# A decoder layer on one core: memory between attention and mixer laid out anew, the mixer's first weights split beside the last projection tiles, the down projection's maxima queued behind other reads

## Chip, cores and metric

One core of one Trainium2 chip. The metric is the device time in microseconds of one execution. Its engines are TensorE (PE, with its weight loads as PEld), VectorE (DVE), ScalarE (ACT), GpSimd (POOL) and SyncE (SP); DMA transfers are issued here from SP's and ACT's queues. Each engine takes its instructions in the order in which they were laid down when the program was built.

## The reference

One layer on x (2048 tokens, 1024 wide), all float32: a token mixer of four head groups (RWKV-7, mLSTM, sliding-window attention, forgetting attention), whose outputs are concatenated and projected, and then a gated MLP. The change lies between the last attention and the end of the MLP:

```python
y = jnp.concatenate([y_a, y_b, y_c, y_d], axis=-1).astype(dt)
x = x + _rmsnorm(y @ w_out[l], norm_mix_post[l]).astype(dt)
h = _rmsnorm(x, norm_ffn_pre[l]).astype(dt)
gate, up = jnp.split(h @ ffn_w_up[l], 2, axis=-1)
gate = _causal_dwconv(gate, ffn_conv_w[l], ffn_conv_b[l])
f = jax.nn.gelu(gate, approximate=True) * up
x = x + _rmsnorm(f @ ffn_w_down[l], norm_ffn_post[l]).astype(dt)
```

w_out is 1024 x 1024, ffn_w_up 1024 x 5632, ffn_w_down 2816 x 1024, the convolution has width 3.

## The kernel before

Every float32 operand of a large product is split into two float16 parts (a leading part and a residual, scaled by a power of two taken from its largest magnitude), and a product is three products of parts. The largest magnitude of a weight block needs a maximum along the rows (VectorE) and one over the partitions (GpSimd, partition_all_reduce).

**Attention (fox).** 16 items (head, token chunk of 512) in sequence. An item has a front (products of queries and keys, row maxima fmx on VectorE) and a back (products again, exponentials on ACT, residuals fhl on VectorE or GpSimd, products with the values). The front of an item is interleaved with the back of the one before it. Chunk c needs c+1 key blocks (ka and kb), loaded from ACT's queue into a ring of buffers, whose number is the first argument of fox_pools: 8 in the second half. The last four items are those of chunk 3.

**Output projection.** o_tiles(c) does the four tiles of 128 tokens of chunk c: o_front loads y, takes its maximum, splits it and transposes it by DMA (yt); o_back makes 96 products with Wo, normalises, adds x, normalises again and transposes the result into U2[c], the float16 parts of the mixer's input (V0 to V3 in the trace). Tiles of chunks 0 and 1 run beside attention; the last four tiles need the last four items.

**Mixer.** The up projection uses a two by two scheme with seven products of blocks instead of eight: combine(p) builds the sums and differences of the blocks of U2 of two chunks, split into float16 parts, T0 for p = 0 and T1 for p = 1. A unit of it (eight in each) is 4 sums on GpSimd, 4 subtractions and a residual on VectorE and a cast on ACT. For each of the 22 weight blocks j, up_weights(j) loads 1 MB (raw), takes its maximum, and makes four sums on GpSimd (S); up_split makes the float16 parts Wup (two buffers, w_n). ffn_up(p, j) is a pass: 84 products of 512 columns into three banks (psa, psb, psc, each double), evictions on ACT and VectorE (line 1656), convolution, GELU, the product F on GpSimd, and a write to DRAM (fD). The order of the passes is (0,0), (0,1), (1,0), (1,1), then (0,j), (1,j) for j = 2 to 21. up_weights also loads the block j of the down projection's weights (rd) and takes its maximum mD (line 1620).

**Down projection.** It reloads weights (wdr) and F (fr), splits both and makes 2112 products; the scale of all weights comes from the 22 maxima mD.

**Order and memory.** The planner of the tile framework orders each engine's instructions greedily in a simulated timeline: an instruction goes as soon as its inputs and its memory are free, earlier program text first. issue_after(mark) keeps instructions of the same engine behind the instruction mark. Pools are stacked from both ends of a partition's memory; a new tile waits for the old tiles over whose bytes it lies.

Of the kernel before, what the change touches and what calls it, by code (L numbers as in the profile page):

```python
# [9 lines left out]
F32 = mybir.dt.float32  # L10
F16 = mybir.dt.float16
# [11 lines left out]
NC = T // C  # L23
# [116 lines left out]
class Trunk:  # L140
# [794 lines left out]
    def stage2(self):  # L935
        with ExitStack() as ck, ExitStack() as co:
            self.cr_.close()
            self.fk = self.pool(ck, "fk")
            items = [[(h, c) for h in hs] for c, hs in ((0, (0, 1)), (1, (0, 1)), (0, (2, 3)), (1, (2, 3)), (2, range(4)), (3, range(4)))]
            with ExitStack() as cf:  # L940
                self.fox_pools(cf, 5, 3, 5, 2)
                self.fox_setup()
                self.fox_items = iter(items[0] + items[1] + items[2])
                self.fox(3, True)
                self.fill_heads(1)
                self.fox(3)
# [510 lines left out]
    def o_setup(self, ctx):  # L1457
        nc = self.nc
        self.U2 = [self.u2p.tile([P, 2, KT, C], F16, name=f"V{c}") for c in range(2)] + [None] * (NC - 2)
        self.so = self.small = self.pool(ctx, "small_o", bufs=2, side="right")  # L1460
        wp = self.pool(ctx, "wo", side="right")
        self.pso2 = self.pool(ctx, "ps_g", bufs=2, space=PSUM, side="right")
        self.row(wp, "post1")
        self.grow2 = self.gain_row(wp, 1)
# [7 lines left out]
        self.ow = self.pool(ctx, "ow", bufs=1, side="right")  # L1472
        self.of = None
# [71 lines left out]

    def combine(self, p, buf, T):
# [4 lines left out]
        for k in range(4):  # L1551
            for t in range(0, C, W):
# [4 lines left out]
                for o, a, b in ((0, 1, 0), (1, 3, 1), (3, 3, 0), (2, 2, 3)):  # L1557
                    nc.vector.tensor_tensor(out=x[:, o], in0=x[:, a], in1=x[:, b], op=ALU.subtract)  # L1558
                nc.scalar.copy(out=T[:, :, 0, k, ts], in_=x)
                nc.vector.tensor_tensor(out=T[:, :, 1, k, ts], in0=x, in1=T[:, :, 0, k, ts], op=ALU.subtract)  # L1560


    def stage_n(self):
# [4 lines left out]
        with ExitStack() as ctx:  # L1568
            self.small = self.sn
            self.raw = self.pool(ctx, "raw_n", bufs=1)  # L1570
            self.wp = self.pool(ctx, "w_n", bufs=2)
            self.wk = self.pool(ctx, "wk_n", bufs=2)
            self.psw = self.pool(ctx, "ps_w", bufs=2, space=PSUM)
            tp = self.pool(ctx, "t1_n", side="right")
            W = {}
# [7 lines left out]
            self.combine(1, lambda n: self.U2[1][:, n % 2, 0:4].rearrange("p k t -> p (k t)").bitcast(F32).rearrange("p (o t) -> p o t", o=4), self.Tc[1])  # L1583
            for j in range(2):
                if j == 1:
                    W[2] = self.up_weights(2)
                mark = self.ffn_up(1, j, W[j])
            W[2] = self.up_split(W[2], mark)
            for j in range(2, NF):
# [3 lines left out]
                if j + 1 < NF:  # L1593
                    W[j + 1] = self.up_split(W[j + 1], mark)
# [3 lines left out]
            self.late()  # L1598
        self.cb.close()
        self.c2.close()  # L1600
        self.ffn_down()

    def up_weights(self, j):

        nc = self.nc
        R = self.raw.tile([P, 4, C], F32, name="raw", tag="raw")
# [4 lines left out]
        S = self.raw.tile([P, 3, C], F32, name="S")  # L1611
        gt = lambda o, x, y, op: nc.gpsimd.tensor_tensor(out=o, in0=x, in1=y, op=op)
# [3 lines left out]
        gt(S[:, 2], R[:, 3], S[:, 0], ALU.subtract)  # L1616

        d = self.wk.tile([P, D], F32, name="rd", tag="rd", bufs=1)
        nc.sync.dma_start(out=d, in_=self.A["w_dn"][j])
        nc.vector.tensor_reduce(out=self.mD[:, j:j + 1], in_=d, axis=AX.X, op=ALU.max, apply_absolute_value=True)  # L1620
        return R, S, m

    def up_split(self, w, mark):

# [3 lines left out]
        with ExitStack() as c:  # L1628
# [3 lines left out]
            nc.vector.tensor_tensor(out=m[:, 2:3], in0=un, in1=self.ug[:, 1:2], op=ALU.mult)  # L1632
        W = self.wp.tile([P, 2, 7, C], F16, name="Wup")
        for o, x in ((slice(0, 4), R), (slice(4, 7), S)):
# [4 lines left out]
    def ffn_up(self, p, j, w):  # L1639

        nc, wk = self.nc, self.wk
        W, un = w
        B, Tc = self.U2[2 * p:2 * p + 2], self.Tc[p]
# [3 lines left out]
        rhs.update({f"T{t}": lambda b, k, o=o: Tc[:, o, b, k] for o, t in enumerate((1, 3, 4, 2))})  # L1647

# [8 lines left out]

        gb = wk.tile([P, 2 * C + 2], F32, name="gb")
        up = wk.tile([P, 2, C], F32, name="up")
        X = wk.tile([P, C], F32, name="X", bufs=1)  # L1660
        g2 = gb[:, C + 2:]
# [25 lines left out]
        F = wk.tile([P, 2, C], F32, name="F")  # L1687
        t = F.rearrange("p c n -> p (c n)")
# [27 lines left out]
    def ffn_down(self):  # L1716

        nc = self.nc
        with ExitStack() as ctx:
            wa = self.pool(ctx, "wa_d")  # L1720
            Wd = [None] * 3 + [wa.tile([P, 2, D], F16, name=f"Wd{j}") for j in range(3, 19)]
# [8 lines left out]
            Wd = [wb.tile([P, 2, D], F16, name=f"Wd{j}") for j in range(3)] + Wd[3:] + [wb.tile([P, 2, D], F16, name=f"Wd{j}") for j in range(19, NF)]  # L1730

# [58 lines left out]
    def run(self):  # L1790
        self.cu, self.cr_, self.cf, self.c2, self.cb = (ExitStack() for n in range(5))
        self.setup()
# [23 lines left out]
```

## Time and profile before

| | us |
|---|---|
| median of 3 runs | 3048.73 |
| lowest and highest | 3047.21 and 3053.03 |
| profiled execution | 3054.69 |
| its span, first to last instruction | 3052.8 |
| TensorE busy in the span | 2745.3 (90%) |
| VectorE / ScalarE / GpSimd busy | 1729.3 / 1038.4 / 802.6 |

The profile is of one execution. In a row of the trace an instruction has its start, its length, its line and its tiles as out<-in; in brackets stands how long its engine was idle before it and what ended that. A stretch is written as start:end in microseconds from the first instruction.

### The profile page before, as it was taken

To read this page: it belongs to the slowest core of one execution; us is meant where nothing else is said; L and a number is where in the kernel's file an instruction comes from. 1 tells how busy PE (TensorE), PEld (TensorE's weight loads), DVE (VectorE), ACT (ScalarE), POOL (GpSimd) and SP (SyncE) were. 2 spreads that over 40 slices of the span, in tenths; PEclk is the share of its full clock that TensorE was granted. 3 is DMA by queue.
4 is the path that set the end of the run, shared out by engine and by line. 5 is a ranking of instruction groups with operands and counts; after the bars stand their busy time and mean duration, and the time that the engine had idled before them with its cause. 6 is when DMAs were issued, how large, how long until landed. Compare 5 with 4: busy or idle time off the path is not lost.

```text
span 3052.8 us, 45125 instructions
## 1 busy us (share of the span) xinstructions
PE 2745.3 (90%) x17401; PEld 1654.0 (54%) x17401; DVE 1729.3 (57%) x3517; ACT 1038.4 (34%) x1844; POOL 802.6 (26%) x979
## 2 busy tenths in 40 slices
PE   5998898999968997899976668999999998999998
PEld 2455776777757785676755223444444443444443
DVE  7645675676756554576766665666666565623021
ACT  4423222444532224465663222222222222612020
POOL 2432221333233331122234322322223222010110
PEclk9998998998988997899987789999999999999999
DMA  9512333345532375674534331111111112823120
GB/s 260 122 59 71 94 92 96 90 117 130 133 110 80 97 196 159 136 164 119 126 87 111 104 122 58 58 70 60 55 56 56 56 55 75 287 98 100 45 86 21
DMA packets 341399, 313.69 MB, mean 103 GB/s; under 512 B 217600, under 2 KB 271232, under 8 KB 338368
## 3 DMA queue, kind: packets, MB, share of 16 engines
q1 hardware_dynamic: 265856, 238.42, 27.9%
q10 hardware_dynamic: 75328, 72.39, 8.2%
q8 instruction: 137, 2.24, 0.3%
q14 instruction: 78, 0.64, 0.1%
HBM read 187.86 MB, written 89.56 MB: 91 GB/s over the span
## 4 chain that ended last, share of the span: by engine, by line
PE 28%; DVE 9%; issue 7%; DMA 2%; POOL 2%; ACT 2%; ACTq 0%; POOLq 0%; SPq 0%; DVEq 0%
PE psd L1751 10%; PE psb L1653 8%; PE psc L1653 5%; PE psa L1653 4%; DVE Wup L1636 2%; DVE F L1691 1%; DVE F L1690 1%; DMA rd<-in_w_dn 1%; ACT F L1689 1%; DVE mF L1695 1%; DVE up L1656 1%; DVE gb L1656 1%; DVE mD L1620 1%; DVE V L1558 0%; DVE xs L1558 0%
## 5 line engine op out<-in xcount | busy, mean ns | idle before, releaser
L1653 PEld LDWEIGHTS <-Wup 128*128 128x128 f16 x3696 | 362.5, 99 | 525.2 <-issue 55.3
L1751 PE MATMUL psd<-Wd,f 128*128 128x512 f16 x2112 | 459.5, 381 | 10.3 <-ACT f L1744 6.1
L1653 PE MATMUL psb<-T,Wup 128*128 128x512 f16 x1584 | 373.0, 385 | 37.7 <-DVE up L1656 33.9
L1751 PEld LDWEIGHTS <-f 128*128 128x128 f16 x2112 | 207.3, 98 | 262.5 <-issue 8.9
L1653 PE MATMUL psa<-V,Wup 128*128 128x512 f16 x1056 | 252.8, 383 | 34.3 <-ACT Wup L1635 25.8
L308 PE MATMUL psg<-Wo,yt 128*128 128x256 f16 x512 | 146.0, 285 | 53.4 <-DMA yt<-hl 49.3
L1656 DVE SCALAR_TENSOR_TENSOR up<-psb,wm,X 128x512 f32<-128x512 f32 x88 | 65.9, 748 | 199.9 <-PE psb L1653 199.7
L1668 ACT ACTIVATE X<-psa,wm 128x512 f32<-128x512 f32 x44 | 30.2, 687 | 432.4 <-DVE up L1656 421.0
L299 PE MATMUL psf<-U,hi_fm 128*128 128x256 f16 x576 | 163.0, 283 | 0.0
L298 PE MATMUL psf<-U,hi_fm 128*128 128x256 f16 x576 | 163.0, 283 | 0.0
L300 PE MATMUL psf<-U,lo_fm 128*128 128x256 f16 x576 | 162.9, 283 | 0.0
L310 PE MATMUL psg<-Wo,yt 128*128 128x256 f16 x512 | 143.8, 283 | 10.6 <-DMA yt<-hl 10.6
L309 PE MATMUL psg<-Wo,yt 128*128 128x256 f16 x512 | 146.1, 285 | 0.0
L1759 DVE TENSOR_SCALAR od<-psd,sf 128x512 f32<-128x512 f32 x16 | 12.0, 749 | 232.6 <-PE psd L1751 228.1
L309 PE MATMUL psf<-lo_fv,U 128*128 128x256 f16 (+1 forms) x512 | 135.5, 272 | 2.7 <-DVE lo_fv L286 2.7
L308 PE MATMUL psf<-hi_fv,U 128*128 128x256 f16 (+1 forms) x512 | 135.5, 273 | 1.4 <-DVE gt L873 1.4
L1366 DVE TENSOR_REDUCE fmx<-psf 128x1 f32<-128x512 f32 (+3 forms) x160 | 95.9, 606 | 70.9 <-PE psf L1363 50.3
L310 PE MATMUL psf<-hi_fv,U 128*128 128x256 f16 (+1 forms) x512 | 135.7, 273 | 0.0
L1400 ACT ACTIVATE fP<-psf,ln2k 128x512 f32<-128x512 f32 (+3 forms) x160 | 98.3, 627 | 85.5 <-PE psf L1398 37.4
L1653 PE MATMUL psc<-T,Wup 128*128 128x512 f16 x528 | 127.2, 381 | 0.0
L1693 POOL TENSOR_TENSOR F<-F,up 128x1024 f32<-128x1024 f32 x44 | 103.3, 2348 | 68.9 <-ACT F L1692 61.2
L1653 PE MATMUL psc<-V,Wup 128*128 128x512 f16 x528 | 121.2, 379 | 0.0
(452 smaller groups left out, 5929.4 us busy)
## 6 DMA issues: line engine op xcount, KB each, us to landing
raw<-in_w_up SPq DMA_DIRECT2D x22, 1024.0 KB
fD<-F SPq DMA_DIRECT2D x44, 512.0 KB
fr<-fD SPq DMA_DIRECT2D x88, 256.0 KB
rd<-in_w_dn SPq DMA_DIRECT2D x22, 512.0 KB
wdr<-in_w_dn ACTq DMA_DIRECT2D x22, 512.0 KB
zin<-zR SPq DMA_DIRECT2D x80, 128.0 KB
ka<-kA ACTq DMA_DIRECT2D x40, 256.0 KB
wst<-in_w_cm SPq DMA_DIRECT2D x17, 512.0 KB
```

Source lines behind the costliest of these rows:

```text
L298: nc.tensor.matmul(ps[:, sl], lhsT=hi[:, k, n0:n0 + nn], rhs=uh[:, k, sl], start=k == 0, stop=False)
L299: nc.tensor.matmul(ps[:, sl], lhsT=hi[:, k, n0:n0 + nn], rhs=ul[:, k, sl], start=False, stop=False)
L300: nc.tensor.matmul(ps[:, sl], lhsT=lo[:, k, n0:n0 + nn], rhs=uh[:, k, sl], start=False, stop=k == KT - 1)
L308: nc.tensor.matmul(ps, lhsT=uh[:, k, sl], rhs=hi[:, k, n0:n0 + nn], start=k == 0, stop=False)
L309: nc.tensor.matmul(ps, lhsT=uh[:, k, sl], rhs=lo[:, k, n0:n0 + nn], start=False, stop=False)
L310: nc.tensor.matmul(ps, lhsT=ul[:, k, sl], rhs=hi[:, k, n0:n0 + nn], start=False, stop=k == KT - 1)
L1366: nc.vector.tensor_reduce(out=mx[:, i, b:b + 1], in_=ps[:, :n], axis=AX.X, op=ALU.min)
L1400: nc.scalar.activation(out=e[:, o:], in_=ps[:, o:], func=AF.Exp, scale=-1.0, bias=self.ln2k)
L1653: nc.tensor.matmul(ps, lhsT=W[:, a, n, ks], rhs=rhs[u](b, k), start=first and k == 0 and i == 0, stop=k == 3 and i == 2, skip_group_check= ...
L1656: return nc.vector.scalar_tensor_tensor(out=out, in0=ps, scalar=un, in1=x, op0=ALU.mult, op1=ALU.add)
L1693: nc.gpsimd.tensor_tensor(out=t, in0=t, in1=up.rearrange("p c n -> p (c n)"), op=ALU.mult)
L1751: nc.tensor.matmul(ps, lhsT=f[:, a, sl], rhs=Wd[j][:, b, ns], start=j == 0 and k == 0, stop=j == NF - 1 and k == 2)
```

## The change

- Attention's second half has 7 key buffers instead of 8.
- T0 becomes two tiles of half the size. T0a lies beside V0 and V1, and its half of combine(0) stands in the program after o_tiles(1), ahead of the last four items of attention; T0b and its half come after the last projection tile. T1 becomes two tiles too.
- The projection's pools change places: rows post1 and g2, then the work pool ow, then Wo lowest.
- A pool n_a holds the first weight buffer Wup0, raw and S; it is opened before the last eight tiles. up_weights(0) and up_split(0) stand behind o_tiles(3) in the program, ahead of the mixer's pools. Wup1, X, up, gb, F and rd are fixed tiles, used in turn, instead of pool slots.
- The load and maximum of a down weight block move out of up_weights into down_max(j, mark), called after the pass (1, j-1) (for j = 0 and 1 after (1, j)); the maximum stands behind an eviction of that pass (mark).
- The row post2 is loaded when the down projection begins, not when attention ends. Some of the down projection's weight tiles change pool.

```diff
-                self.fox_pools(cf, 8, 4, 6, 4)
+                self.fox_pools(cf, 7, 4, 6, 4)
...
                     if c <= 2:
                         self.o_tiles(c - 1)
+                    if c == 2:
+                        self.combine(0, lambda n: self.ow.tile([P, 4, W], F32, name="xs"), range(2))
...
-            self.row(keep, "post2")
...
-            self.Tc = [u2b.tile([P, 4, 2, 4, C], F16, name="T0")]
+            self.Tc[0].append(u2b.tile([P, 4, 2, 2, C], F16, name="T0b"))
             self.tails = {}
-            for c in range(2, NC):
-                self.o_tiles(c)
-                if c == 2:
-                    self.combine(0, lambda n: self.ow.tile([P, 4, W], F32, name="xs"), self.Tc[0])
+            na = self.pool(self.cn, "n_a")
+            self.Wt = [na.tile([P, 2, 7, C], F16, name="Wup0")]
+            self.raw = na.tile([P, 4, C], F32, name="raw"), na.tile([P, 3, C], F32, name="S")
+            self.o_tiles(2)
+            self.o_tiles(3)
+            w = self.up_weights(0)
+            self.combine(0, lambda n: self.ow.tile([P, 4, W], F32, name="xs"), range(2, 4))
+            self.W = {0: self.up_split(0, w, None)}
...
+        self.Tc = [[self.u2p.tile([P, 4, 2, 2, C], F16, name="T0a")], []]
         self.so = self.small = self.pool(ctx, "small_o", bufs=2, side="right")
+        rp = self.pool(ctx, "wor", side="right")
+        self.row(rp, "post1")
+        self.grow2 = self.gain_row(rp, 1)
+        self.ow = self.pool(ctx, "ow", bufs=1, side="right")
         wp = self.pool(ctx, "wo", side="right")
...
-            for j in range(2):
-                W[j] = self.up_weights(j)
-                W[j] = self.up_split(W[j], None)
-            self.Tc.append(tp.tile([P, 4, 2, 4, C], F16, name="T1"))
+            W[1] = self.up_split(1, self.up_weights(1), None)
+            self.Tc[1] += [tp.tile([P, 4, 2, 2, C], F16, name=f"T1{i}") for i in range(2)]
...
                 mark = self.ffn_up(1, j, W[j])
-            W[2] = self.up_split(W[2], mark)
+                self.down_max(j, mark)
+            W[2] = self.up_split(2, W[2], mark)
+            self.down_max(2, mark)
...
                 mark = self.ffn_up(1, j, W[j])
+                if j + 1 < NF:
+                    self.down_max(j + 1, mark)
...
+    def down_max(self, j, mark):
+
+        nc, d = self.nc, self.rd
         nc.sync.dma_start(out=d, in_=self.A["w_dn"][j])
-        nc.vector.tensor_reduce(out=self.mD[:, j:j + 1], in_=d, axis=AX.X, op=ALU.max, apply_absolute_value=True)
+        with self.tc.issue_after(mark.ins):
+            nc.vector.tensor_reduce(out=self.mD[:, j:j + 1], in_=d, axis=AX.X, op=ALU.max, apply_absolute_value=True)
...
             fp = self.pool(ctx, "f_d")
+            self.row(fp, "post2")
```

## Rows read from the trace of the kernel before

**Rows 1.** Windows: stretch, length, busy us (instructions) of each engine, clock, DMA.
```profile
core 0: us, PE busy (x) PEld busy (x) DVE busy (x) ACT busy (x) POOL busy (x), PEclk, DMA share, GB/s
1408.00:1577.40 169.40, 156.46 (x1305) 117.50 (x1303) 119.91 (x230) 112.03 (x209) 48.42 (x41) 0.98 0.38 98
1577.40:1686.00 108.60, 61.08 (x481) 49.99 (x480) 66.54 (x107) 35.70 (x57) 47.99 (x52) 0.76 0.55 128
...
1702.20:1823.90 121.70, 84.30 (x336) 34.72 (x336) 84.64 (x95) 27.37 (x27) 37.54 (x46) 0.85 0.31 105
1823.90:1870.20 46.30, 33.61 (x144) 14.63 (x145) 23.02 (x26) 9.54 (x9) 8.04 (x8) 0.85 0.27 91
1870.20:2573.80 703.60, 697.90 (x3218) 313.13 (x3216) 428.93 (x438) 196.16 (x191) 203.35 (x186) 1.00 0.16 58
```
**Rows 2.** Timeline of TensorE, 1700 to 1870: start, us, line, operation, [idle before, releaser].
```profile
1702.19 1.03 PE L1653 MATMUL psa<-V,Wup 128*128 128x512 f16 x2 [16.20 <-ACT Wup L1635]
...
1733.73 1.04 PE L1653 MATMUL psa<-V,Wup 128*128 128x512 f16 x2 [7.70 <-ACT Wup L1635]
1777.00 4.61 PE L1653 MATMUL psb<-T,Wup 128*128 128x512 f16 x12 [15.16 <-DVE up L1656]
...
1815.18 4.29 PE L1653 MATMUL psb<-T,Wup 128*128 128x512 f16 x12 [3.23 <-DVE up L1656]
...
1857.48 5.28 PE L1653 MATMUL psb<-T,Wup 128*128 128x512 f16 x12 [12.66 <-DVE up L1656]
```
**Rows 3.** Timeline of ACT: the first split of weight block 0.
```profile
1700.14 2.00 ACT L1635 ACTIVATE Wup<-raw,p 128x2048 f16<-128x2048 f32 x1
```
**Rows 4.** Waits of VectorE, 1577 to 1870: us in total, times, longest.
```profile
DVE V L1558 <- POOL V L1556: 30.3, 4, 11.7
DVE mD L1620 <- DMA rd<-in_w_dn: 29.0, 10, 14.8
```
**Rows 5.** Line 1620: ns min/median/max, first and last; timeline of VectorE.
```profile
L1620 DVE TENSOR_REDUCE mD<-rd x22: 1204/1213/1221, 1708.7 to 1860.4; 128x1 f32<-128x1024 f32 x22
...
1790.81 3.02 DVE L1560 TENSOR_TENSOR T<-V,T 128x1024 f16<-128x1024 f32 x1
...
1855.55 1.22 DVE L1620 TENSOR_REDUCE mD<-rd 128x1 f32<-128x1024 f32 x1 [14.82 <-DMA rd<-in_w_dn]
```
**Rows 6.** Tile Wup: ns min/median/max of the splits, first and last start.
```profile
L1635 ACT ACTIVATE Wup<-raw,p x22: 1985/1987/2002, 1700.1 to 2527.9; 128x2048 f16<-128x2048 f32 x22
...
L1636 DVE SCALAR_TENSOR_TENSOR Wup<-S,p,Wup x22: 1801/3441/3451, 1709.8 to 2533.5; 128x1536 f16<-128x1536 f32 x22
```
**Rows 7.** Timeline of SP's queue: the last transposes of the projection.
```profile
1671.84 30.05 SPq L322 DMA_TRANSPOSE V<-hl  x6
```
**Rows 8.** Tile xs, the first combination: ns min/median/max, first and last start.
```profile
L1556 POOL TENSOR_TENSOR xs<-V x32: 662/667/1660, 1313.0 to 1660.6; 128x256 f32<-128x256 f16 x32
L1558 DVE TENSOR_TENSOR xs<-xs x32: 408/425/2382, 1402.5 to 1664.5; 128x256 f32<-128x256 f32 x32
...
L1560 DVE TENSOR_TENSOR T<-xs,T x8: 1218/1222/1226, 1580.4 to 1666.1; 128x1024 f16<-128x1024 f32 x8
```
**Rows 9.** Timeline of GpSimd: the maximum over partitions of weight block 0.
```profile
1606.50 0.38 POOL L1610 PARTITION_ALL_REDUCE wm<-wm  x1 [5.83 <-issue]
1614.09 1.26 POOL L1612 TENSOR_TENSOR raw<-raw 128x512 f32<-128x512 f32 x1 [7.22 <-issue]
...
1616.77 1.27 POOL L1612 TENSOR_TENSOR S<-raw,S 128x512 f32<-128x512 f32 x1
```
**Rows 10.** Timeline of ACT's queue: key loads of the last item; QB ends a front.
```profile
1512.32 0.33 ACTq L1347 DMA_DIRECT2D ka<-kA  x1
...
1520.45 0.36 ACTq L1347 DMA_DIRECT2D ka<-kA  x1
...
1526.08 0.58 ACT L1380 CAST QB<-psf 2x512 fp32r<-2x512 f32 x1 [3.03 <-PE psf L1379]
```
**Rows 11.** Timeline of ACT at the start of the down projection.
```profile
2595.11 1.15 ACT L1736 ACTIVATE Wd<-wdr,sd 128x1024 f16<-128x1024 f32 x1 [8.40 <-DMA wdr<-in_w_dn]
```

More of the change, by code (lines that the diff above doesn't have):

```diff
@@ L1471, in o_setup @@
             self.Wo.append((t[:, 0], t[:, 1], self.uo[:, n:n + 1]))
-        self.ow = self.pool(ctx, "ow", bufs=1, side="right")
         self.of = None
@@ L1544, in o_back, with combine @@
         return nxt
-    def combine(self, p, buf, T):
+    def combine(self, p, buf, ks):
         nc = self.nc
         B = [self.U2[2 * p + c][:, :, 4 * k:4 * k + 4] for c in range(2) for k in range(2)]
-        for k in range(4):
+        for k in ks:
+            T = self.Tc[p][k // 2]
             for t in range(0, C, W):
@@ L1558, in combine @@
                     nc.vector.tensor_tensor(out=x[:, o], in0=x[:, a], in1=x[:, b], op=ALU.subtract)
-                nc.scalar.copy(out=T[:, :, 0, k, ts], in_=x)
-                nc.vector.tensor_tensor(out=T[:, :, 1, k, ts], in0=x, in1=T[:, :, 0, k, ts], op=ALU.subtract)
+                nc.scalar.copy(out=T[:, :, 0, k % 2, ts], in_=x)
+                nc.vector.tensor_tensor(out=T[:, :, 1, k % 2, ts], in0=x, in1=T[:, :, 0, k % 2, ts], op=ALU.subtract)
     def stage_n(self):
@@ L1569, in stage_n @@
             self.small = self.sn
-            self.raw = self.pool(ctx, "raw_n", bufs=1)
-            self.wp = self.pool(ctx, "w_n", bufs=2)
-            self.wk = self.pool(ctx, "wk_n", bufs=2)
+            self.Wt.append(self.pool(ctx, "n_w").tile([P, 2, 7, C], F16, name="Wup1"))
+            one = lambda n, shape: self.pool(ctx, "n_" + n).tile(shape, F32, name=n)
+            two = lambda n, shape: [one(n + str(i), shape) for i in range(2)]
+            self.X = one("X", [P, C])
+            self.up, self.gb, self.F = two("up", [P, 2, C]), two("gb", [P, 2 * C + 2]), two("F", [P, 2, C])
+            self.rd = one("rd", [P, D])
+            self.nup = 0
             self.psw = self.pool(ctx, "ps_w", bufs=2, space=PSUM)
             tp = self.pool(ctx, "t1_n", side="right")
-            W = {}
+            W = self.W
             self.late = None
-            for j in range(2):
-                W[j] = self.up_weights(j)
-                W[j] = self.up_split(W[j], None)
-            self.Tc.append(tp.tile([P, 4, 2, 4, C], F16, name="T1"))
+            W[1] = self.up_split(1, self.up_weights(1), None)
+            self.Tc[1] += [tp.tile([P, 4, 2, 2, C], F16, name=f"T1{i}") for i in range(2)]
             for j in range(2):
                 mark = self.ffn_up(0, j, W[j])
-            self.combine(1, lambda n: self.U2[1][:, n % 2, 0:4].rearrange("p k t -> p (k t)").bitcast(F32).rearrange("p (o t) -> p o t", o=4), self.Tc[1])
+            self.combine(1, lambda n: self.U2[1][:, n % 2, 0:4].rearrange("p k t -> p (k t)").bitcast(F32).rearrange("p (o t) -> p o t", o=4), range(4))
             for j in range(2):
@@ L1593, in stage_n @@
                 if j + 1 < NF:
-                    W[j + 1] = self.up_split(W[j + 1], mark)
+                    W[j + 1] = self.up_split(j + 1, W[j + 1], mark)
                 mark = self.ffn_up(1, j, W[j])
+                if j + 1 < NF:
+                    self.down_max(j + 1, mark)
                 if j == NF - 1:
@@ L1598, in stage_n @@
             self.late()
+        self.cn.close()
         self.cb.close()
@@ L1605, in up_weights @@
         nc = self.nc
-        R = self.raw.tile([P, 4, C], F32, name="raw", tag="raw")
+        R, S = self.raw
         nc.sync.dma_start(out=R.rearrange("p s n -> p (s n)"), in_=self.A["w_up"][j])
@@ L1610, in up_weights @@
         nc.gpsimd.partition_all_reduce(m[:, 1:2], m[:, 0:1], P, RMAX)
-        S = self.raw.tile([P, 3, C], F32, name="S")
         gt = lambda o, x, y, op: nc.gpsimd.tensor_tensor(out=o, in0=x, in1=y, op=op)
@@ L1616, in up_weights, with up_split @@
         gt(S[:, 2], R[:, 3], S[:, 0], ALU.subtract)
-        d = self.wk.tile([P, D], F32, name="rd", tag="rd", bufs=1)
+        return R, S, m
+    def down_max(self, j, mark):
+        nc, d = self.nc, self.rd
         nc.sync.dma_start(out=d, in_=self.A["w_dn"][j])
-        nc.vector.tensor_reduce(out=self.mD[:, j:j + 1], in_=d, axis=AX.X, op=ALU.max, apply_absolute_value=True)
-        return R, S, m
-    def up_split(self, w, mark):
+        with self.tc.issue_after(mark.ins):
+            nc.vector.tensor_reduce(out=self.mD[:, j:j + 1], in_=d, axis=AX.X, op=ALU.max, apply_absolute_value=True)
+    def up_split(self, j, w, mark):
         nc = self.nc
@@ L1632, in up_split @@
             nc.vector.tensor_tensor(out=m[:, 2:3], in0=un, in1=self.ug[:, 1:2], op=ALU.mult)
-        W = self.wp.tile([P, 2, 7, C], F16, name="Wup")
+        W = self.Wt[j % 2]
         for o, x in ((slice(0, 4), R), (slice(4, 7), S)):
@@ L1639, in ffn_up @@
     def ffn_up(self, p, j, w):
-        nc, wk = self.nc, self.wk
+        nc = self.nc
         W, un = w
+        n2 = self.nup % 2
+        self.nup += 1
         B, Tc = self.U2[2 * p:2 * p + 2], self.Tc[p]
@@ L1646, in ffn_up @@
         rhs = {"B11": lambda b, k: B[0][:, b, k], "B21": lambda b, k: B[0][:, b, 4 + k], "B22": lambda b, k: B[1][:, b, 4 + k]}
-        rhs.update({f"T{t}": lambda b, k, o=o: Tc[:, o, b, k] for o, t in enumerate((1, 3, 4, 2))})
+        rhs.update({f"T{t}": lambda b, k, o=o: Tc[k // 2][:, o, b, k % 2] for o, t in enumerate((1, 3, 4, 2))})
         def product(ps, n, u, first):
@@ L1656, in add @@
             return nc.vector.scalar_tensor_tensor(out=out, in0=ps, scalar=un, in1=x, op0=ALU.mult, op1=ALU.add)
-        gb = wk.tile([P, 2 * C + 2], F32, name="gb")
-        up = wk.tile([P, 2, C], F32, name="up")
-        X = wk.tile([P, C], F32, name="X", bufs=1)
+        gb, up, X, F = self.gb[n2], self.up[n2], self.X, self.F[n2]
         g2 = gb[:, C + 2:]
@@ L1686, in ffn_up @@
             nc.gpsimd.tensor_copy(out=self.tails[j], in_=gb[:, 2 * C:])
-        F = wk.tile([P, 2, C], F32, name="F")
         t = F.rearrange("p c n -> p (c n)")
@@ L1720, in ffn_down @@
             wa = self.pool(ctx, "wa_d")
-            Wd = [None] * 3 + [wa.tile([P, 2, D], F16, name=f"Wd{j}") for j in range(3, 19)]
+            Wd = [None] * 3 + [wa.tile([P, 2, D], F16, name=f"Wd{j}") for j in range(3, 18)]
             s0 = self.pool(ctx, "s0_d")
@@ L1729, in ffn_down @@
             sd, sf = self.sd, self.sf
-            Wd = [wb.tile([P, 2, D], F16, name=f"Wd{j}") for j in range(3)] + Wd[3:] + [wb.tile([P, 2, D], F16, name=f"Wd{j}") for j in range(19, NF)]
+            Wd = [wb.tile([P, 2, D], F16, name=f"Wd{j}") for j in range(3)] + Wd[3:] + [wb.tile([P, 2, D], F16, name=f"Wd{j}") for j in range(18, NF)]
             def weights(j):
@@ L1790, in run @@
     def run(self):
-        self.cu, self.cr_, self.cf, self.c2, self.cb = (ExitStack() for n in range(5))
+        self.cu, self.cr_, self.cf, self.c2, self.cb, self.cn = (ExitStack() for n in range(6))
         self.setup()
```

2 lines of the change are left out of this document (removed).

## Prediction

> **What bounds the kernel now.** I read the windows first: busy time and granted clock by stretch [rows 1]. The reader is to see where TensorE is not full. From 1870.2 to 2573.8 us it is busy 697.9 of 703.6 us at clock 1.00, and 3218 products take 697.9 us, 0.217 us each: nothing is to be had there. Before 1577.4 (attention) it is busy 156.5 of 169.4 us. Between the two lies the weak place: 1577.4 to 1870.2 us, 292.8 us with 179.0 us of products, part of them at the lower granted clock (a mean of 0.76 to 0.85 of full speed, between the two levels of 1.2 and 2.4 GHz). Three holes make it: the tail of the projection (47.5 us idle), a hole with no product at all (16.2 us), and the first passes of the mixer (50.1 us idle).
>
> Then TensorE's own timeline names what ended each wait [rows 2]. The hole of 16.20 us ends with the first weights of the mixer (ACT, Wup), one of 7.70 us with the second weights; 15.16, 3.23 and 12.66 us end with a VectorE eviction (up, line 1656). Behind the hole, ACT's row [rows 3]: the first weights' maximum is known at 1606.9 [rows 9], but their conversion starts at 1700.14, after the last projection tile. In the compiled program's map of on-chip memory the weight pool w_n spans 101.9 to 129.9 KiB and the projection's pool ow 115.5 to 151.5 KiB, so the weights wait for its y and yt tiles; row and map agree. Behind the late evictions VectorE's rows and waits [rows 4, 5]: all 22 maxima mD lie between 1708.7 and 1861, ten times VectorE stood still for their reads (29.0 us, 14.8 at the longest), and the evictions TensorE wants are queued behind them.
>
> **Removed: the hole before the mixer.** After the change the first weight buffer lies over attention's memory, which is free at 1577.4, and load, maximum and split (2.0 us for the larger part on ACT, 1.8 to 3.4 for the smaller on VectorE [rows 6]) run among the last projection tiles. The second buffer still lies over Wo, free with the last projection product (E, 1686.0 before); it is wanted only after 84 products, 18.2 us, longer than its split. The first pass needs V0 and T0 alone. Both waits, 16.2 and 7.7 us, should go.
>
> **What is late next: T1.** The four passes 1702.2 to 1823.9 hold 336 products, 72.9 us at 0.217, and took 121.7. T1, the second combination, is due when half of them are done. It ended at 1793.8 [rows 5], 108 us after E. It can't start before the last tile's transposes, which ended E+16 [rows 7]. It needs 8 units; from the first combination's rows [rows 8] a unit costs 4 x 0.667 us on GpSimd, 4 x 0.425 + 1.222 on VectorE. VectorE: 8 x 2.92 = 23.4 us, plus two passes at 428.93/(3218/84) = 11.2 us each: 45.8 us from E. GpSimd: 21.3 us, one maximum over partitions with three of its four sums, from 1606.50 - 5.83 = 1600.7 to 1618.0, 17.3 us [rows 9] (two such lay here before; the one for the second weights can now run earlier): 38.6 us from about E+8, before its share of the two passes. The lower end is E+46, the upper E+62 (E+16, six units of 2.92, GpSimd's 17.3 and one pass's 11.2, one after the other); I take E+58, nearer the upper, because GpSimd's stall stands in these rows and VectorE waited 30.3 us for GpSimd's sums [rows 4]. After T1 there are 156 products of the four passes left (the first pass over the second half has 12 it can run ahead): 33.8 us, E+92; with 4 us for the wait on an eviction and the third weights (3.23 us on the eviction alone before [rows 2]), the fifth pass starts at E+96. Before it started at 1823.9, E+138. **Term: -42 us** (ends -38 and -54).
>
> **Removed: the stalls behind mD.** In 1823.9 to 1870.2, 144 products (31.2 us) took 46.3; the 12.66 us in it ends with an eviction queued behind an mD that waited 14.82 us [rows 2, 5]. With each mD behind an eviction of its own pass, and its read a pass ahead, **-13 us** (0 to -15). Added instead: VectorE has one mD (1.21 us) for each weight block in the steady stretch, where it is busy 61% and TensorE is not waiting: +2 (0 to 20 x 1.21 = 24). What is queued behind a late one there is the eviction of psc, with a second bank behind it; SP issues the read after the previous maximum, some 36 us ahead, with the raw weights and fD writes on the same queue. The third block's mD follows the second's at once and may wait for its read, inside that bound.
>
> **Moved: half of combine(0) into attention.** Twelve subtractions (four lie there already, from 1402.5) and four residuals: 12 x 0.425 + 4 x 1.222 = 10.0 us of VectorE, 8 us of GpSimd, into 169.4 us where VectorE is busy 71% and TensorE idle 12.9 us. Ends 0 and +10.0; I take +3, since TensorE leads there. Queued behind it are attention's row maxima and residuals (fmx, fhl).
>
> **Removed: one key buffer.** The last four items hold four key blocks each; eight buffers hold two items. Loads of one item are issued as blocks come free, 8.1 us apart, the last at 1520.45, 5.6 us before the front that wants them [rows 10]. With seven, each load goes one release later: the fourth comes some 8 us into that front, which wants it at about that time. Three fronts, each 0 to 12 us (one release of 8.1 and a landing, say 12): 0 to +36; I take +4, since the front is interleaved with another item's products. A gain is excluded: the same work with fewer buffers.
>
> **The projection's tail.** 108.6 us for 61 us of products. Half the combination leaves it (12 subtractions, 4 residuals, 12 sums, beside the four of each that lie in attention already); the first split and, if the queues let it, the second weights' maximum with its 17.3 us of GpSimd come in, and every tile needs GpSimd three times. The two are about equal: 0, ends -13 and +14.
>
> **The end.** The row post2 (0.5 MB) is read when the down projection begins, on ACT's queue ahead of its weight loads, and the buffers for later loads lie over the mixer's last F and gb. Before, ACT waited 8.40 us there for a weight read [rows 11]. 0 to +8; I take +2. The Trainium skill, "DMA: Bandwidth & Descriptors", section "Issuing engines are not separate DMA queues", says that DMAs of all issuers share the same 16 engines; so moving the row to another queue would not spare it, and by that the term would be nearer its upper end, the sum -38 instead of -44. No row of before shows this read at this place.
>
> **Sum.** -42 -13 +2 +3 +4 +0 +2 = **-44 us**. The profiled execution took 3054.69 us (span 3052.8), 6.0 above the median of 3048.73; the sum is made against it and carried to the median: **3005 us**. With the terms near their ends its own range is 2985 to 3020.
>
> **The rivals.**
> *Only the mD stalls go.* If the planner or GpSimd's 17.3 us stall keeps the first split late, or T1 comes as late after the mixer's start as before, what is left is 13 and some 10 us of mD work in the four passes: about 3026 (3018 to 3040). For it: GpSimd's stalls are not touched, and T1 has the same 8 units. Against it: the hole's cause is memory, and that moves.
> *More goes.* The first pass has 36 products that need nothing from the projection's memory; in the tail's idle 47.5 us TensorE can run them ahead, and with the tail's -13 and T1 at its early end the sum is -78: 2971.
> *Attention pays, slower.* VectorE and GpSimd work moved beside attention, and the fourth key block late in three fronts: +36, +10, and if each of the 12 moved subtractions takes the longest 2.38 us seen instead of 0.42 [rows 8], 12 x 1.96 = +23.5. Together +69.5 against -51 from the other terms: about 3067. It decides if attention's last product, at 1577.4 now, moves past 1628. For it: fronts and backs share in-order queues. Against it: TensorE is 92% busy there, with work to put in between. The Trainium skill, "SBUF — State Buffer", section "Who interferes with whom", says that a VectorE instruction with two inputs in SBUF contends with a GpSimd instruction that reads SBUF; the spread from 0.408 to 2.382 us in [rows 8] agrees with that. By this rule the moved subtractions meet attention's GpSimd residuals, which is the +23.5.
> *The change doesn't do what it says.* The first split still lands after the last tile and mD still heads the queue: 3049.
>
> **How the numbers follow.** Forecast 0.50, only mD 0.20, more 0.14, attention pays 0.09, nothing 0.07. The range 2970 to 3042 takes in the first two and most of the third, about 0.82. A measurement of this kernel can tell 0.2%, 6 us, from no change. Faster: 0.50 + 0.20 + 0.14 = 0.84; same 0.07; slower 0.09.
>
> **What would show it.** Right: the first Wup conversion before the last projection product, and no gap over 3 us between that product and the mixer's first; mD rows spread to 2540 us with waits near zero; the fifth pass at E+96; the wait that is left ends with T1; attention's end within 10 us of 1577. Wrong: a gap on Wup as long as before; T1 later than E+62; mD waits on rd in the steady stretch; fronts of attention that wait for ka or kb; or a tail of the projection over 120 us, where the second weights' maximum holds GpSimd.

## The result and the profile after

The changed kernel takes 3023.89 us (median of 14 runs) beside 3046.73 for the kernel before on the same chip (14 runs): ratio 0.9926, interval 0.9911 to 0.9940. It is faster by 22.8 us, half of the 44 forecast. The profiled execution took 3021.11 us, its span 3019.3.

The work ahead of attention is untouched, yet attention's first product with the values starts anywhere from 1109.1 to 1129.2 us in the fourteen profiles of this study (1118.1 before, 1109.1 after). So stages are compared from that product on, always from the start of one product to the start of another: attention from its first to its last value product, the tail from there to E, the start of the last projection product, and the rest as the table says. Figures as E+16 are microseconds behind E in the same profile; a difference of 0.1 us is rounding.

| stage, us | before | after | forecast of the difference |
|---|---|---|---|
| attention | 459.1 | 452.7 | +7 |
| tail of the projection, to E | 108.5 | 116.7 | 0 |
| E to the fifth mixer pass | 138.2 | 112.8 | -42 |
| fifth pass to the mixer's last products | 749.6 | 736.7 | -11 |
| from there to the down projection's first product | 6.5 | 14.6 | +2, with the next |
| down projection | 463.3 | 467.1 | |

The differences are -6.4, +8.2, -25.4, -12.9, +8.1 and +3.8, together -24.6. The windows of after (columns as in [rows 1]) are attention's end, tail, first passes, rest of the mixer, start of the down projection:

```profile
core 0: us, PE busy (x) PEld busy (x) DVE busy (x) ACT busy (x) POOL busy (x), PEclk, DMA share, GB/s
1392.00:1561.80 169.80, 152.97 (x1249) 113.93 (x1248) 125.03 (x236) 113.73 (x209) 57.81 (x53) 0.96 0.36 95
1561.80:1678.70 116.90, 74.19 (x520) 54.34 (x517) 59.48 (x92) 33.65 (x52) 40.72 (x40) 0.77 0.48 121
1678.70:1791.30 112.60, 73.86 (x301) 30.77 (x300) 72.52 (x85) 33.59 (x39) 41.91 (x45) 0.87 0.18 58
1791.30:2528.40 737.10, 731.22 (x3360) 327.59 (x3360) 467.31 (x476) 204.56 (x198) 206.25 (x194) 1.00 0.20 71
2528.40:2565.00 36.60, 15.73 (x56) 6.28 (x57) 19.73 (x28) 17.00 (x19) 3.09 (x3) 0.75 0.67 248
```

From the fifth pass on TensorE is as full as it was only behind 1870.2 before. The tail and the first passes are still the weak place: 42.7 and 38.7 us without a product. TensorE's timeline there (columns as in [rows 2]):

```profile
1600.72 1.03 PE L1672 MATMUL psa<-V,Wup 128*128 128x512 f16 x2 [8.74 <-ACT Wup L1652]
...
1682.57 0.60 PE L1672 MATMUL psa<-V,Wup 128*128 128x512 f16 x2 [3.77 <-ACT Wup L1652]
...
1717.55 4.33 PE L1672 MATMUL psa<-V,Wup 128*128 128x512 f16 x12 [12.22 <-ACT X L1685]
...
1752.34 0.59 PE L1672 MATMUL psb<-T,Wup 128*128 128x512 f16 x1 [8.13 <-ACT T L1567]
...
1761.69 0.58 PE L1672 MATMUL psb<-T,Wup 128*128 128x512 f16 x1 [4.00 <-ACT T L1567]
...
1791.31 1.03 PE L1672 MATMUL psa<-V,Wup 128*128 128x512 f16 x2 [4.53 <-ACT Wup L1652]
```

Mixer products run ahead in the tail from 1600.72, and behind E the hole of 16.20 us [rows 2] is 3.77. But T1 still ends waits (8.13 and 4.00), and a new one of 12.22 us has come in. GpSimd's timeline shows what is behind both, the maxima over partitions (PARTITION_ALL_REDUCE) of the first three weight blocks:

```profile
1589.37 0.38 POOL L1625 PARTITION_ALL_REDUCE wm<-wm  x1 [5.83 <-issue]
1597.38 1.25 POOL L1626 TENSOR_TENSOR raw<-raw 128x512 f32<-128x512 f32 x1 [7.64 <-issue]
...
1617.22 0.38 POOL L1625 PARTITION_ALL_REDUCE wm<-wm  x1 [5.91 <-issue]
1624.68 0.59 POOL L231 TENSOR_TENSOR ot<-rsq,mhalf 128x1 f32<-128x1 f32 x1 [7.08 <-issue]
...
1697.92 0.38 POOL L1625 PARTITION_ALL_REDUCE wm<-wm  x1 [5.96 <-issue]
1705.75 1.25 POOL L1626 TENSOR_TENSOR raw<-raw 128x512 f32<-128x512 f32 x1 [7.45 <-issue]
1706.97 2.33 POOL L1548 TENSOR_TENSOR xr<-xr,o 128x1024 f32<-128x1024 f32 x1
```

Two lie in the tail; a projection tile's square root (ot, line 231) stands behind the second, although VectorE had its input ready at 1610.8. The third, of the third weights, stands between the last tile's VectorE product (o, 1692.78 to 1694.05) and its residual sum (line 1548) at 1706.97. Before, that sum came 6.1 us behind E, here 28.5, and T1 is made from that tile. The timelines of VectorE and, below it, of ACT show both waiting with it:

```profile
1692.78 1.27 DVE L1547 SCALAR_TENSOR_TENSOR o<-o,ot,r_post 128x1024 f32<-128x1024 f32 x1
...
1710.88 0.15 DVE L230 TENSOR_SCALAR rsq<-ss 128x1 f32<-128x1 f32 x1 [14.11 <-ACT hl L330]
...
1716.04 0.74 DVE L1675 SCALAR_TENSOR_TENSOR up<-psb,wm,X 128x512 f32<-128x512 f32 x1
```
```profile
1709.70 1.06 ACT L330 ACTIVATE hl<-xr 128x1024 bf16<-128x1024 f32 x1 [20.47 <-POOL xr L1548]
...
1716.82 0.69 ACT L1685 ACTIVATE X<-psa,wm 128x512 f32<-128x512 f32 x1 [1.96 <-DVE up L1675]
```

The eviction of psb at 1716.04 is queued on VectorE behind the last tile's steps, and X behind it: that is the 12.22 us.

mD is as meant: 22 maxima from 1774.1 to 2496.8, one wait of 1.4 us, where [rows 4] had 29.0. The start of the down projection in ACT's timeline and, below it, in GpSimd's:

```profile
2524.49 0.34 ACTq L347 DMA_DIRECT2D r_post<-in_prow  x1
2524.86 1.42 ACTq L1773 DMA_DIRECT2D xo<-x2buf  x3
...
2535.91 1.34 ACT L1761 ACTIVATE f<-fr,sf 128x512 f16<-128x512 f32 x2 [5.36 <-DVE sf L1730]
2539.61 1.06 ACT L1708 ACTIVATE F<-F 128x1024 f32<-128x1024 f32 x1 [2.37 <-DVE F L1707]
2540.74 0.72 ACT L1761 ACTIVATE f<-fr,sf 128x512 f16<-128x512 f32 x1
2541.37 1.13 ACT L1753 ACTIVATE Wd<-wdr,sd 128x1024 f16<-128x1024 f32 x1
```
```profile
2534.48 0.38 POOL L1723 PARTITION_ALL_REDUCE mm<-mm  x1 [9.13 <-issue]
```

The row post2 and three reads of x2 (2 MB) go out just ahead, GpSimd's maximum of mm is preceded by 9.13 us instead of 6.10 before, and the first weights (Wd0) are converted last, some 6 us behind the scale. TensorE waits 14.2 us for them (6.1 before).

### The profile page after: what moved, and what is told of

Same layout as the page of the kernel before. It is cut to its first block, busy times and chain, and to the rows that moved or that the text cites. A ratio compares the mean times of both kernels' runs of the same rounds, so it can differ in the third digit from the quotient of the medians.

```text
span 3019.3 us, 45043 instructions
## 1 busy us (share of the span) xinstructions
PE 2746.7 (91%) x17401; PEld 1655.2 (55%) x17401; DVE 1726.0 (57%) x3517; ACT 1038.3 (34%) x1844; POOL 802.9 (27%) x979
## 4 chain that ended last, share of the span: by engine, by line
PE 61%; DVE 14%; issue 9%; DMA 7%; ACT 4%; POOL 3%; SPq 1%; ACTq 0%; POOLq 0%; DVEq 0%
PE psd L1768 10%; PE psb L1672 9%; PE psc L1672 5%; PE psa L1672 5%; PE psf L298 2%; PE psf L299 2%; PE psf L300 2%; DVE Wup L1653 2%; PE psf L308 1%; PE psf L310 1%; PE psf L309 1%; PE psb L662 1%; PE pss L1253 1%; PE pso L1415 1%; PE psb L682 1%
## 5 line engine op out<-in xcount | busy, mean ns | idle before, releaser
L1672 PE MATMUL psb<-T,Wup 128*128 128x512 f16 x792 | 189.7, 382 | 17.9 <-ACT T L1567 13.5
L1415 PE MATMUL pso<-FV,fhl 128*128 128x129 f16 x1088 | 99.8, 227 | 15.3 <-POOL fhl L1409 7.6
```

Source lines behind the costliest of these rows:

```text
L1415: nc.tensor.matmul(po[i // 2][:, i % 2 * 129:i % 2 * 129 + 129], lhsT=h[:, n, i * P:(i + 1) * P], rhs=self.V2[:, s, hp], start=s == 0 and ...
L1672: nc.tensor.matmul(ps, lhsT=W[:, a, n, ks], rhs=rhs[u](b, k), start=first and k == 0 and i == 0, stop=k == 3 and i == 2, skip_group_check= ...
```

## Experiments

Runs were made on several chips, so each time is given as its ratio to the kernel before on the same chip. After has 0.9926 (0.9911 to 0.9940) from its own runs and was not run again beside the experiments; two ratios whose intervals overlap are not told apart. Comments behind # in the diffs explain and are not in the code; ... stands for lines left out. Each profile is one execution; tail and mixer together are 996.3 us before and 966.2 after, start and products of the down projection together 469.8 and 481.7.

**The third maximum.** In up_weights:

```diff
-        nc.vector.tensor_reduce(out=m[:, 0:1], ...)
+        with ExitStack() as c:
+            if mark is not None:   # j = 2: an eviction of pass (1, 0)
+                c.enter_context(self.tc.issue_after(mark.ins))
+            nc.vector.tensor_reduce(out=m[:, 0:1], ...)
```

> The changed kernel, with the third weight block's maximum held behind a VectorE eviction of the third mixer pass. Theory A (in the trace of after, GpSimd's maximum over partitions for the third weights, 1690.7 to 1712, lies between the last tile's VectorE product at 1692.78 and its residual sum at 1706.97, and so starts T1 about 13 us late): the residual sum follows its product at once, T1 ends about E+71 instead of E+84, the fifth pass starts about 10 us sooner, and the time falls from 3023.9 to 3011 to 3016. Rival B (VectorE's own queue sets T1's end, or the third weights now come too late): 3022 to 3030.

Measured 0.9907 (0.9893 to 0.9921). The residual sum came at E+14.4 (28.5), T1 ended at E+70.8 (84.4), as theory A has it. The fifth pass gained less, E+104.8 (112.8), since now the third weights are late, as TensorE's timeline says:

```profile
1792.05 1.03 PE L1675 MATMUL psa<-V,Wup 128*128 128x512 f16 x2 [9.63 <-ACT Wup L1655]
```

Tail and mixer took 959.0, 7 less. That the third maximum made T1 late is shown; of its 13.6 us, some 6 turn into another wait. The 8 to 13 us that theory A forecast were not reached, and by the time alone the run is not told apart from after.

**All three maxima off GpSimd.** In up_weights, for j < 3:

```diff
-        nc.gpsimd.partition_all_reduce(m[:, 1:2], m[:, 0:1], P, RMAX)
+        mm = self.pmax(m[:, 0:1], 1)   # transpose, maximum, spread by a product
...
```

> The changed kernel, with the maxima over partitions of the first three weight blocks taken on TensorE (transpose, VectorE maximum, a product that spreads it) instead of on GpSimd. Theory A (GpSimd, in order, stands about 13 us beside each of the three maxima, and the projection's tail and T1 queue behind it): the tail of 116.9 us falls to about 97 and T1 starts 13 us sooner, 2990 to 3004. Rival B (the tail is a chain of loads, transposes and evictions that GpSimd's stalls only fill): only what holding the third maximum alone gives, 3011 to 3018.

Measured 0.9825 (0.9812 to 0.9838), 2998.62 us. Tail 97.5, mixer 838.0, together 935.5: 30.7 us less than after. Theory A holds. GpSimd's timeline has the last tile's residual sum 4.2 us behind E, which is 1666.9 here:

```profile
1667.21 0.15 POOL L1686 MEMSET gb<- 128x2 f32 x2 [9.32 <-PE psg L310]
1669.08 0.55 POOL L231 TENSOR_TENSOR ot<-rsq,mhalf 128x1 f32<-128x1 f32 x1 [1.73 <-DVE rsq L230]
1671.09 4.33 POOL L1548 TENSOR_TENSOR xr<-xr,o 128x1024 f32<-128x1024 f32 x1 [1.46 <-DVE o L1547]
```

TensorE's timeline has the maximum of the first weights (lines 209 and 212) right behind the last projection product:

```profile
1666.98 0.27 PE L209 MATMUL psg<-c,wm 128*1 128x128 f32 x1
1667.63 0.38 PE L212 MATMUL psg<-c,pm 1*128 1x1 f32 x2 [0.37 <-DVE pm L211]
1670.67 1.03 PE L1678 MATMUL psc<-T0a,Wup 128*128 128x512 f16 x2 [2.67 <-ACT Wup L1658]
```

So the first split (1668.62) is no longer beside the projection, and yet the hole ahead of the mixer's first product is only 2.67 us. That the tail is shorter only because the split left it is ruled out further below, where the split is put back and the tail stays at 98.9.

**The reads of post2 and x2.** Both behind the eleventh conversion of weights:

```diff
-            self.row(fp, "post2")
...
+                    with self.tc.issue_after(a.ins):   # a: the conversion of Wd10
+                        self.row(fp, "post2")
...
-                nc.scalar.dma_start(out=x, in_=self.x2[r])
+                with self.tc.issue_after(self.mark3.ins):
+                    nc.scalar.dma_start(out=x, in_=self.x2[r])
```

> The changed kernel, with the reads of post2 and of x2 for the closing sums held behind the eleventh conversion of the down projection's weights. Theory C (the 2 MB read at 2524.5 to 2532 stand before what the start of the down projection needs, and lengthen GpSimd's maximum from 6.1 to 9.1 us): 3 to 8 us back, 3016 to 3021. Rival D (the start is late because Wd0 lies over the second weight buffer and is converted behind f and F): no change, 3022 to 3025.

Measured 0.9918 (0.9898 to 0.9938); the time can't tell it from after. The stage can: start and products of the down projection took 477.9, 3.8 less, the low end of theory C, and in GpSimd's timeline the maximum is back at 6.13 us:

```profile
2556.00 0.38 POOL L1723 PARTITION_ALL_REDUCE mm<-mm  x1 [6.13 <-issue]
```

**The place of Wd0 to Wd2.** Their buffers and those of Wd15 to Wd17 exchanged:

```diff
-            Wd = [None] * 3 + [wa.tile(...) for j in range(3, 18)]
+            Wd = [wa.tile(...) for j in list(range(3, 15)) + [0, 1, 2]]   # the last three lie over Wup0
...
```

> The changed kernel, with the buffers of Wd0 to Wd2 exchanged with those of Wd15 to Wd17, so that they lie over the first weight buffer, which is free before the last pass ends. Theory D (the conversion of Wd0 stood at 2541.37, 5.9 us behind the scale at 2535.5, because its memory is the buffer that the last pass reads): Wd0 is converted right behind the scale and the first product comes 4 to 6 us sooner, 3017 to 3021. Rival C (the reads of post2 and x2 are the cause): no change, 3022 to 3025.

Measured 0.9897 (0.9884 to 0.9909). Start and products took 469.6, all of the 12 us back: 4.5 of them ahead of the first product and the rest while the products run, most of that in waits (after has one of 4.52 us). The reads still stand ahead of GpSimd's maximum (9.67 us). ACT's timeline has Wd0 first:

```profile
2549.08 1.15 ACT L1754 ACTIVATE Wd<-wdr,sd 128x1024 f16<-128x1024 f32 x1 [5.70 <-DVE sd L1728]
2550.14 1.32 ACT L1762 ACTIVATE f<-fr,sf 128x512 f16<-128x512 f32 x2
```

Theory D holds: the change put Wd0 over the weight buffer that the last pass still reads, and so behind f and F. With Wd0 in place the reads cost nothing that the stage shows.

**Seven key buffers alone**, in the kernel before:

```diff
-                self.fox_pools(cf, 8, 4, 6, 4)
+                self.fox_pools(cf, 7, 4, 6, 4)
```

> The kernel before with seven key buffers instead of eight, nothing else. My price in the forecast: +4 us (0 to +36). The trace of after, where attention did not take longer (452.7 us from its first value product to its last, 459.1 before), speaks for 0: 3044 to 3050. If the fourth key block is late in three fronts: 3055 to 3080.

Measured 0.9975 (0.9955 to 0.9995). Attention took 461.2 (459.1): no cost that the profile shows. Tail and mixer took 988.6 (996.3), although nothing was changed in them, and no cause was found. All of it lies ahead of the fifth mixer pass (238.3 beside 246.7 us for tail and first passes; 750.2 and 749.5 behind). So differences of up to 8 us in tail and first passes against the one profile of before are not to be read.

**mD alone**, in the kernel before (down_max and its calls as in the change):

```diff
-        nc.sync.dma_start(out=d, in_=self.A["w_dn"][j])
-        nc.vector.tensor_reduce(out=self.mD[:, j:j + 1], ...)
+    def down_max(self, j, mark):
+        nc.sync.dma_start(out=d, in_=self.A["w_dn"][j])
+        with self.tc.issue_after(mark.ins):
+            nc.vector.tensor_reduce(out=self.mD[:, j:j + 1], ...)
...
```

> The kernel before with the down projection's maxima mD alone moved: each read a pass ahead and held behind an eviction of its own pass. Theory of the forecast (the stalls behind mD cost the 15.1 us by which the stretch 1824 to 1870 was long, while the first passes wait for weights and T1 anyway): 13 to 15 us, 3031 to 3034. Rival (the other stalls, 29.0 us in all, also held T1's units on VectorE, so T1 comes sooner too): 20 to 30 us, 3016 to 3027, and then most of what the whole change gave is this part's.

Measured 0.9928 (0.9903 to 0.9954). Tail and mixer 980.1, 16.2 less than before; T1 ended at E+95.6 (108.1), yet the fifth pass started at E+134.8 (138.2), and 12.0 of the gain lies behind it. Those 12.0 us stand clear, since before and the run with seven buffers agree there; the other 4 lie within what these two differ by. The stages speak for the forecast's theory. The ratio is as low as the whole change's: with the down projection mD alone gives 16.6 us, the whole change, which pays 11.9 there, 18.2.

**The half combination back into the tail**, in the changed kernel:

```diff
-                    if c == 2:
-                        self.combine(0, ..., range(2))
...
-            self.combine(0, ..., range(2, 4))
+            self.combine(0, ..., range(4))
```

> The changed kernel with the whole first combination after the last projection tiles, as before, instead of half of it inside attention. If the tail is bound by GpSimd and VectorE and attention hides the half: slower by 8 to 15 us, 3032 to 3039. If the tail has room for it, or attention pays for it as much: 3021 to 3027.

Measured 0.9945 (0.9920 to 0.9970). Tail and mixer 968.9 (966.2): 2.7 us more, which is nearer the second case but can't be told from nothing. The runs of the late reads and of the exchanged buffers, which leave the combination in attention, have 967.5 and 969.2.

**The first split not beside the projection**, in the changed kernel: the first maximum behind the last tile's last VectorE product (nmark), with up_weights as in the first experiment:

```diff
-            w = self.up_weights(0)
+            w = self.up_weights(0, self.nmark)
...
```

> The changed kernel with the first weight block's maximum held behind the last projection tile's last VectorE product, so that the first split is no longer beside the projection, while the memory stays laid out anew. Forecast's theory (the hole before the mixer and the wait for the second weights, 16.2 and 7.7 us, are what the early split removes): 15 to 25 us slower, 3039 to 3049. Rival (the early maxima stall GpSimd in the tail by about as much as the hole costs): within 6 us of 3023.9, the tail some 10 to 20 us shorter and a hole of about 30 us before the mixer's first product.

Measured 0.9917 (0.9889 to 0.9944). The rival holds: the tail falls from 116.7 to 89.8 (more than the 10 to 20 us that it said), the mixer rises from 849.5 to 875.7, together 965.5 (966.2). The hole is there in TensorE's timeline, and half of it is GpSimd's maximum, as its timeline below shows:

```profile
1704.03 1.03 PE L1675 MATMUL psa<-V,Wup 128*128 128x512 f16 x2 [28.26 <-ACT Wup L1655]
```
```profile
1692.43 0.38 POOL L1628 PARTITION_ALL_REDUCE wm<-wm  x1 [5.99 <-issue]
1700.69 1.25 POOL L1629 TENSOR_TENSOR raw<-raw 128x512 f32<-128x512 f32 x1 [7.88 <-issue]
```

**Both mends**, the maxima on TensorE and the exchanged Wd buffers:

> The changed kernel with both mends: the maxima of the first three weight blocks on TensorE, and Wd0 to Wd2 over the first weight buffer. If the two are independent their gains add: tail and mixer some 30 us shorter than in after, the start of the down projection and its first products some 10 us, ratio to the kernel before 0.977 to 0.981. If the second mend only moves a wait into the down projection: 0.981 to 0.984.

Measured 0.9804 (0.9782 to 0.9825), 2989.68 us. Tail and mixer 934.0, down projection 472.0: 32.2 and 9.7 us less than after, where the mends alone gave 30.7 and 12.1, so in the stages the gains add. By the time alone the run is not told apart from the one with the maxima on TensorE (0.9812 to 0.9838).

**Both mends, the first split early again**:

```diff
+            w = self.up_weights(0)
             self.o_tiles(3)
-            w = self.up_weights(0)
```

> As the run with both mends, and the first block's load, maximum and sums stand ahead of the last four projection tiles in program order, so that the first split lies beside them again, now without GpSimd's stall. Theory (once the maximum costs 1.5 us and not 13, the first split behind the last tile leaves a hole of only 3.9 us): 0 to 6 us faster than the run with both mends. Rival (TensorE, in order, waits inside the tail for the maximum, and the split takes ACT and VectorE from the tiles): 0 to 8 us slower.

Measured 0.9787 (0.9768 to 0.9805), 2985.9 us. Tail and mixer 935.1, as without: no worth in the early split here either. The tail is 98.9 us, 18 less than in after with the split in the same place, so some 18 us of the tail were GpSimd's stalls. TensorE waits 3.05 us for the maximum inside the tail. The ratio's interval overlaps that of the run before.

**Both mends, and the maximum of mm on TensorE**, in f_scale for p = 0:

```diff
-        nc.gpsimd.partition_all_reduce(mm[:, 3:3 + n], mm[:, 0:n], P, RMAX)
+        am = self.pmax(mm[:, 0:n], n)
...
```

> As the run with both mends, and the maximum over partitions of mm, which the start of the down projection waits for, on TensorE too. Theory: the stretch from the mixer's last product to the first of the down projection falls from about 10 us to 6, the time by 3 to 5 us. Rival (weights and values read there come no sooner): no change within 2 us.

Measured 0.9786 (0.9765 to 0.9806), 2984.76 us. The first product of the down projection comes 5.0 us behind the mixer (9.4), but start and products together take 470.2 (472.0): what was saved at the start is waited for behind it. The time is not told apart from the two runs above.

**The maxima on TensorE alone, in the kernel before**, the same three steps as in the second experiment:

> The kernel before with the maxima over partitions of its first three weight blocks on TensorE, nothing else moved. If GpSimd's stalls cost before about what they cost after: 20 to 30 us faster than before, ratio 0.990 to 0.9935. If it was the change that put them where they hurt (before, the waits for memory and for mD end later anyway): 0 to 8 us, ratio 0.9975 to 1.000.

Measured 0.9885 (0.9864 to 0.9907), 3014.02 us beside 3053.37: more than either case said, and more than the whole change gives (0.9911 to 0.9940). Tail 99.3, mixer 854.7, together 42 us less than before, 11.2 of it behind the fifth pass. The hole that memory makes is still there in TensorE's timeline:

```profile
1691.23 1.03 PE L1661 MATMUL psc<-T,Wup 128*128 128x512 f16 x2 [14.93 <-ACT Wup L1643]
```

## Why the prediction was right in sign and off in size

3023.9 us lies inside the range of 2970 to 3042, but above the 2985 to 3020 that the forecast gave its own case. By the time alone it is in the band of the rival "only the mD stalls go" (3018 to 3040), and mD alone measures nearly the same ratio, 0.9928. The stages say that this is not what happened: the first split was early, T1 ended 24 us sooner behind E, and other stages took part of that back. What the rival had right is its reason, that GpSimd's stalls are not touched.

**The hole (right in itself, empty in effect).** It closed as said, the memory was its cause (it stays in the last run, where the memory is as before), and mixer products ran ahead. But the term that should have carried its price was the tail's, "the two are about equal: 0". The run with the first split held shows the price: without the maxima beside it the tail is 26.9 us shorter, the mixer 26.2 longer. What the early split gained behind E it paid ahead of E, because GpSimd, in order, starts nothing for some 13 us around each maximum and every tile needs it three times. What it hid was in the main the maximum and not the split: with the maximum on TensorE, late and early first splits give 934.0 and 935.1 us.

**T1 (the step that failed).** Forecast E+58 and the fifth pass at E+96, measured E+84.4 and E+112.8; -25.4 instead of -42. The sum did count one maximum in this stretch, the third weights' (the second's was to run earlier, and did), but as GpSimd work beside the units of T1, and it took the last tile's transposes from before, at E+16. The maximum came ahead of them: raw is free once the second split is done, so the planner brought it forward, in front of the last residual sum. The second split, early now, stands on VectorE ahead of the last tile's steps too (the first of them is on oss, its sum of squares). VectorE's timeline and, below it, that of SP's queue in after:

```profile
1682.55 2.35 DVE L1653 SCALAR_TENSOR_TENSOR Wup<-raw,p,Wup 128x2048 f16<-128x2048 f32 x1
1684.82 1.81 DVE L1653 SCALAR_TENSOR_TENSOR Wup<-S,p,Wup 128x1536 f16<-128x1536 f32 x1
1686.55 0.75 DVE L1675 SCALAR_TENSOR_TENSOR gb<-psb,wm,X 128x512 f32<-128x512 f32 x1
...
1688.35 0.15 DVE L1545 TENSOR_TENSOR oss<-oss 128x1 f32<-128x1 f32 x1
```
```profile
1685.52 31.95 SPq L322 DMA_TRANSPOSE V<-hl  x4
```

The issue of the last transposes ends at E+38.9 and not at E+16, with the third maximum held at E+24.7. From there T1 took 45.4 and 46.1 us, where the sum has 42: the length was priced well, the start was not. Of the 22.7 us by which the start was late, 14.2 are the third maximum's. The other 8.5 stay with it held; oss comes 6 us later behind E than before (9.8 beside 3.7), behind the second split and an eviction, but no run took those away alone. E+96 was reached by no run: with all three maxima away and the first split early T1 ended at E+69.9, the fifth pass at E+98.6.

**mD (right).** -13 and +2 forecast for stalls and steady stretch, -12.9 measured from the fifth pass on; mD alone gave 12.0 there. But this stall had a second cure: the last experiment, with mD where it was, needs 738.4 us for the stretch too. There VectorE still waited 19.0 us for reads of mD, 3.9 at the longest instead of 14.82. Why the reads then meet fewer evictions was not tried.

**Attention (no sign of the +7).** In the fourteen profiles it took 452.7 to 461.8 us, not longer with 7 buffers and the half combination (452.7 to 461.1) than with 8 and without it (458.0 to 461.2). A price of 3 or 4 us would be lost in this spread; the +36 of the upper end is excluded. The longest of the combination's subtractions on xs took 1.19 us, not the 2.38 of [rows 8]; nothing speaks for the rival "attention pays".

**The end (mis-sized).** +2, bounds 0 to +8, measured +11.9. The sum priced the read of post2, and the term named the buffers for later loads without asking whose memory Wd0 gets. The run with the exchanged buffers gives all of it back. The Trainium skill's rule, "DMA: Bandwidth & Descriptors", "Issuing engines are not separate DMA queues", would have put the term near +8 through the reads. Held back, they gave 3.8 us, and with Wd0 in place they cost nothing, so what the rule speaks of was the smaller part.

**What the gain is made of.** Of the 30.1 us in tail and mixer, 12.9 lie behind the fifth pass, where mD alone gave 12.0. The other 17.2 lie in tail and first passes; against the run with seven buffers, which changes nothing there, they are 8.8. Neither the early split nor the half combination shows a worth of its own, and what these 9 to 17 us are made of was not taken apart. The down projection takes 11.9 back.

## What to carry over

A long instruction on an in-order engine has to be priced in every place where the change lets it go, also the next one of its kind, which a freed buffer brings forward. A gap that closes counts only with the stretch from which its work was taken: compare both together. When memory is laid out anew, ask of each tile that is wanted at a stage's start whose last reader it lies over.

## What the runs showed of the hardware

A maximum over partitions on GpSimd shows 0.38 us of work, but in the three rows of after nothing starts on the engine in the 5.8 to 6.0 us before it and in the 7.1 to 7.6 us after it. While the 2 MB for the down projection were read, the stretch ahead of it was 9.13 and 9.67 us, with the reads held back 6.13; why, no run shows. The same result over TensorE took a product of 0.27 us, a maximum on VectorE of 0.28 and products of 0.38 us, and with three of them in place of GpSimd's the tail and the mixer took 30.7 us less in the changed kernel and 42.3 less in the one before, where up to 8 us are within what two profiles differ by.
